# One encoder layer on one core: weight-copy transfers in program order, token quarters of 272, and a last down-product with its depth loop outermost

## The chip, the core and the metric

The kernel runs as one program on one of the cores of a Trainium2 chip. The metric is the device time of one execution in microseconds (us). Before the change it is 1176.99 us, the median of 3 runs (1176.88 to 1177.64). In the tables PE is TensorE, PEld its weight loads, DVE VectorE, ACT ScalarE, POOL GpSimd and SP SyncE, on which most DMAs are issued.

## The reference

One layer over 1024 prompt tokens and 64 tokens of a running stream, 1088 in all, all in float32 (states and small outputs left out):

```
hn = rmsnorm(x, g_pre1); z = hn @ w_in            # 1024 -> gate_a | xa | u | v, 512 each
h  = rg_lru(causal_dwconv(xa, width 4), ...)      # recurrence over tokens, 8 heads
ya = rmsnorm(h * gelu(gate_a), g_out_a)
yb = rmsnorm(spatial_gate(u, layernorm(v), w_s, b_s), g_out_b)
x  = x + rmsnorm(concat(ya, yb) @ w_o, g_post1)   # 1024 -> 1024
up = rmsnorm(x, g_pre2) @ w_up                    # 1024 -> 6144
c  = causal_dwconv(up, width 3)
f  = (gelu(c[..., :3072]) * c[..., 3072:]) @ w_down   # 3072 -> 1024
y  = x + rmsnorm(f, g_post2)
```

## The kernel before

Activations lie transposed: features on the 128 partitions, tokens along the row. Every product is made from three matmuls, since each float32 operand is split into a hi part (a rounded copy, made by ScalarE) and a lo part (the rest, a subtraction on VectorE): hi by hi, hi by lo, lo by hi (`split`, L139 to L144).

The stages on TensorE are, in order: the v product in two passes (tile `vps`, L284 and L290), each over 8 depth blocks k of x; the other three quarters of the input projection (`ps`, L425); the output projection (`ops`, L650) over four token quarters of QW = 274 columns; two pairs of up-projection blocks (`pps`, L775); the other 22 pairs as seven products each (`up`, L906; a product is 24 matmuls, 4 depth blocks by 3 split parts by 2 banks, 3,696 in all), on sums of token quarters; the down projection as seven products of six steps (`dps`, L1067); of those the last product in two column ranges (`lps`, L1067, COLS2). A token row has a gap of 3 columns between the two streams (SG = 1027), for the convolutions. With 4 x 274 = 1096 columns the fourth quarter holds 202 prompt tokens, the gap, 64 sample tokens and 5 columns of nothing: `post1` writes the zeros with GpSimd and cuts its multiplies in two there.

After an up-projection product, ScalarE copies or VectorE adds its two banks into `uraw` (`copy` L920, `add` L925). `gated` makes the convolution and the gate of a pair from it and stores the operand to DRAM (`bd`).

The down projection's weights are w_down blocks and sums of them. Two kinds of sums need w_down[1,0] + w_down[1,1]; that sum is made in DRAM (`sd`) by six copies (L1031, on SP) and six accumulating transfers (L1033, on POOL). They stand in the program text in the loop over the up-projection's pairs, but a scheduler writes each engine's order by when operands are there, and these need nothing: it puts them at the start, on SP between the x loads (`xr`, L323) and the weight loads (`wraw`, L166). A load is followed by a subtraction where the weight is a difference (`wmake`, L1007), then by the split into `whi` and `wlo` (L142). Operands come back from DRAM as `graw` (`bload`) and are split into `gh` and `gl` (`bmake`). The engines' orders are static: each runs its instructions in order.

In the last product each weight tile serves two output blocks. The loop runs over ranges, output blocks m, then the three depth groups kg; weights and operands of a step are made just before (`operand`, L1152). `finish` (L1102) is the work after a column range: a sum of squares over partitions, its inverse root, a broadcast by TensorE, for each of eight blocks a multiply on VectorE (L1112), and a transfer that adds the result onto yT in DRAM (L1113). `finish_last` (L1123) does it for the last range with the gain put in ahead (tile `fg`) and two transfers of four blocks (L1132).

Of the kernel before, what the change touches and what calls it, by code (L numbers as in the profile page):

```python
# [19 lines left out]
QW = 274  # L20
TW = 4 * QW
T = SEQ + DEC
SG = SEQ + GAP
# [20 lines left out]
COLS2 = [(544, 828), (828, 1088)]  # L44
# [23 lines left out]
def layer_kernel(ctx: ExitStack, tc, xT, w_fm, w_v, w_o, w_up, w_down, w_g, w_s, par, bc, yT, small, vn_out):  # L68
# [36 lines left out]
    def qs(q):  # L105
        return slice(q * QW, min(q * QW + QW, T))

    def qw(q):
        return qs(q).stop - q * QW

    def fourth(i, w=QW):
        return slice(i % 4 * QW, i % 4 * QW + w)

    def packed(n, dt, name, w):
        tiles = [big_tile(dt, name=name) for _ in range((n + 3) // 4)]
        return [tiles[i // 4][:, fourth(i, w)] for i in range(n)], tiles

    def v4(t, w=QW):
        return t.rearrange("p (c t) -> p c t", c=4)[:, :, :w]
# [80 lines left out]
    def rstd_tail(head, out):  # L200
# [8 lines left out]
        nc.scalar.activation(out, bp[:, :w], AF.Copy)  # L209
        return bp[:, :w]  # L210
# [349 lines left out]
    def gate_tile_chunks(t):  # L560
        g = big_tile(name="gt")[:, :T]
        h = hst[t]

        def evac(c, ps):
            nc.vector.tensor_tensor(g[:, qs(c)], ps, rbt[:, qs(c)], op=ALU.mult)
            nc.scalar.activation(g[:, qs(c)], g[:, qs(c)], AF.Gelu_apprx_tanh)
            nc.vector.tensor_tensor(h[:, qs(c)], h[:, qs(c)], g[:, qs(c)], op=ALU.mult)
            sat3[c] = acc_tile(qw(c), "sat3")
# [26 lines left out]
    def y_split(c, half):  # L595
        head = rstd_head((sat if half == 0 else sbt)[:, qs(c)], DA, None if half else sat3[c])
        yield
        w = qw(c)
# [3 lines left out]
        for i in range(4):  # L602
            k = half * 4 + i
            y = (hst[i] if half == 0 else s[i])[:, qs(c)]
            nc.vector.scalar_tensor_tensor(y, y, pv("g_out", k), rr, op0=ALU.mult, op1=ALU.mult)
            yh[k, c], yl[k, c] = th[:, fourth(i, w)], tl[:, fourth(i, w)]
            split(yh[k, c], yl[k, c], y)
            if i == 1:
                yield
# [25 lines left out]
    def o_mm(c, gens=()):  # L635
        pss = {}
        w = qw(c)
# [15 lines left out]
        mix, tiles = packed(8, F32, "mix", w)  # L653
# [35 lines left out]
    def load_x(c):  # L689
        xs, tiles = packed(8, F32, "xs", qw(c))  # L690
        for g in range(2):
            nc.sync.dma_start(v4(tiles[g], qw(c)), xT[4 * g:4 * g + 4, :, qs(c)].rearrange("k p t -> p k t"))
        return xs, tiles

    def split_b(name, c, src):
        hi, lo = big_tile(F32R, name="bh"), big_tile(F32R, name="bl")
# [4 lines left out]
    def post1(c, mix, tiles, ssq):  # L701
        w = qw(c)
# [7 lines left out]
        for m in range(KD):  # L710
# [3 lines left out]
            if m % 4 == 3:  # L714
                g = m // 4
                nc.sync.dma_start(yT[:, 4 * g:4 * g + 4, qs(c)], v4(xt[g], w))
            if m == 3:
                yield
        if c == 3:
            n = SEQ - c * QW  # L720
            for t in tiles:
                nc.gpsimd.memset(v4(t)[:, :, n:n + GAP], 0.0)
                nc.gpsimd.memset(v4(t)[:, :, w + GAP:QW], 0.0)
            cuts = ((slice(0, n), slice(0, n)), (slice(n, w), slice(n + GAP, w + GAP)))
        else:
            cuts = ((slice(0, w), slice(0, w)),)
# [7 lines left out]
        for m in range(KD):  # L734
            f = tiles[m // 4][:, fourth(m)]
            for d, g in cuts:
                nc.vector.scalar_tensor_tensor(f[:, g], xs[m][:, d], pv("g_pre2", m), rr2[:, d],
                                               op0=ALU.mult, op1=ALU.mult)
# [26 lines left out]
    def pre_up(n):  # L765
# [4 lines left out]
        def one(i, c):  # L770
# [6 lines left out]
            nc.scalar.activation(raw[i][:, fourth(c)], ps, AF.Copy)  # L777
# [133 lines left out]
    def up_pair(j, hooks=()):  # L911
        xg, xv = big_tile(name="uraw"), big_tile(name="uraw")
        q1, q2, q3, q4 = ([x[:, fourth(2 * c + r)] for c in range(2)]
# [3 lines left out]
        def copy(dst, src):  # L917
            for c in range(2):
                with tc.high_priority(offset=PRI):
                    nc.scalar.activation(dst[c], src[c], AF.Copy)  # L920

        def add(dst, src, p):
            for c in range(2):
                with tc.high_priority(offset=PRI):
                    nc.vector.tensor_tensor(dst[c], src[c], p[c], op=ALU.add)  # L925
# [25 lines left out]
        add(q1, b0, q1)  # L951
# [8 lines left out]
        add(q4, b2, q4)  # L960
# [5 lines left out]
        def last():  # L966
            product(j, 6, b2, False)
            add(q2, b2, q2)
# [17 lines left out]

    def wload(n):
        if n >= NDS:
            return
        p, i = n // 6, n % 6  # L990
# [9 lines left out]
    def wmake(n):  # L1000
        if n >= NDS:
            return
        p, i = n // 6, n % 6
# [17 lines left out]
    for j in range(NPRE, NF):  # L1021
# [39 lines left out]
    def down_mm(dst, cols, n, k, mi, first, last):  # L1061
        hi, lo = wq[n]
        bh, bl = bq[n // 6 * 6 + n % 3 * 2 + k // 2]
# [38 lines left out]
    def finish(cols):  # L1102
# [7 lines left out]
        for m in range(KD):  # L1110
            f = facc[m][:, cols]
            nc.vector.scalar_tensor_tensor(f, f, pv("g_post2", m), rr, op0=ALU.mult, op1=ALU.mult)  # L1112
            nc.gpsimd.dma_start(yT[:, m, cols], f, accum_op=ALU.add)  # L1113
# [3 lines left out]
    fg = {}  # L1117

    def scale_f(m, cols):
        nc.scalar.activation(fg[m // 4][:, m % 4, :], facc[m][:, cols], AF.Copy, scale=pv("g_post2", m))  # L1120

    def finish_last(cols, more):
        w = cols.stop - cols.start  # L1123
        head = rstd_head(ssqt[0][:, cols], D, more)
        scale_f(3, cols)
        rr = tmp_tile(w, name="rrf")
        bp = rstd_tail(head, rr)
        for g, q in ((1, nc.sync), (0, nc.scalar)):
            for m in range(4):
                f = fg[g][:, m, :]  # L1130
                nc.vector.tensor_tensor(f, f, bp, op=ALU.mult)
            nc.gpsimd.dma_start(yT[:, 4 * g:4 * g + 4, cols], fg[g], accum_op=ALU.add)  # L1132

    def down_step(n):
        p, mp, kg = n // 6, n % 6 // 3, n % 3
        for mi in range(2):
# [3 lines left out]
            for k in range(4):  # L1140
                down_mm(dps[m], CC, n, k, mi, kg == 0, kg == 2)
# [9 lines left out]
    last_p = len(DOWN) - 1  # L1151
    def operand(n):  # L1152
        wmake(n + 4)
        bmake(n + 6)
        wload(n + 5)
        bload(n + 7)

    for n in range(6 * last_p):
        if n == 6 * last_p - 6:
# [3 lines left out]
        operand(n)  # L1163
# [3 lines left out]
        if n == 1:  # L1167
            nc.gpsimd.dma_start(small, sm)
    for r, (lo, hi) in enumerate(COLS2):
        cols = slice(lo, hi)  # L1170
        w = hi - lo
        if r == 1:
            for g in range(2):
                fg[g] = big_tile(name="fg")[:, :4 * w].rearrange("p (m t) -> p m t", m=4)
            for m in range(4, KD):
                scale_f(m, cols)
        for m in range(4):
            ps = bank_tile("lps")[:, :w]
            for kg in range(3):
                n = 6 * last_p + m // 2 * 3 + kg  # L1180
                if r == 0 and m % 2 == 0:
                    operand(n)
                for k in range(4):
                    down_mm([ps], [(lo - HT, hi - HT)], n, k, m % 2, kg == 0, kg == 2)
                tick2()
            f = facc_cols(m, lo, hi)
            with tc.high_priority(offset=PRI):
                nc.vector.tensor_tensor(f, ps, f, op=ALU.add)
# [89 lines left out]
```

## Time and profile before

| | us |
|---|---|
| median of 3 runs | 1176.99 |
| the profiled execution | 1176.07 |
| its span, first to last instruction | 1173.9 |
| PE busy (share of the span) | 1132.0 (96%) |
| PEld busy | 1109.0 (94%) |
| DVE busy | 841.0 (72%) |
| ACT busy | 534.2 (46%) |
| POOL busy | 172.0 (15%) |

The trace is of one execution. The shares are means over stages with different limits, so the stages are looked at one by one below. A line of the waits names who was waited for; the chain of waits is followed back from the last instruction; a timeline row may hold several equal instructions (x6), whose time is then from the start of the first to the end of the last.

### The profile page before, as it was taken

The numbers are of one execution on the slowest core, as the hardware profiler recorded it, in microseconds if no ns is written. First come the engines' busy times: TensorE is split into PE (matmuls) and PEld (weight loads), VectorE is DVE, ScalarE is ACT, GpSimd is POOL, SyncE is SP. The second block draws the span as 40 slices with busy tenths as digits, with TensorE's granted clock in tenths as the row PEclk, the third lists the DMA queues.
The fourth block names the chain that finished last, engine by engine and source line by source line (L and its number), as shares of the span: only waits on it lengthen the run. The fifth ranks groups of instructions, "written<-read, shape, count | busy, mean of one in ns | idle before, by whom it ended". The sixth has DMA issues, their size and how long they took to land.

```text
span 1173.9 us, 20616 instructions
## 1 busy us (share of the span) xinstructions
PE 1132.0 (96%) x8420; PEld 1109.0 (94%) x8420; DVE 841.0 (72%) x1363; ACT 534.2 (46%) x876; POOL 172.0 (15%) x291
## 2 busy tenths in 40 slices
PE   6899999999998999999999999999999999999984
PEld 4689999999998999999999999999999999999984
DVE  4568585865678789877877787787789365855753
ACT  4521675645444464444444454454456432523331
POOL 1030001110001113220211111112013000001213
PEclk8999999999999999999999999999999999999987
DMA  9811111140224123221322332232256779555925
GB/s 316 211 54 42 36 37 36 37 129 1 78 96 166 41 79 130 103 103 57 129 99 74 107 114 85 80 130 81 69 207 232 282 256 338 180 213 179 274 31 77
DMA packets 51566, 146.38 MB, mean 125 GB/s; under 512 B 5520, under 2 KB 21392, under 8 KB 51376
## 3 DMA queue, kind: packets, MB, share of 16 engines
q1 hardware_dynamic: 35936, 110.66, 27.3%
q0 software_dynamic: 15312, 34.27, 10.4%
q8 instruction: 66, 1.08, 0.4%
q14 instruction: 28, 0.23, 0.1%
q10 hardware_dynamic: 224, 0.14, 0.0%
HBM read 109.34 MB, written 41.99 MB: 129 GB/s over the span
## 4 chain that ended last, share of the span: by engine, by line
PE 86%; issue 6%; DMA 3%; DVE 2%; POOL 1%; ACT 1%; SPq 0%; POOLq 0%; DVEq 0%; ACTq 0%
PE up L906 40%; PE dps L1067 16%; PE ps L425 12%; PE ops L650 7%; PE pps L775 4%; PE vps L290 2%; DMA xr<-in_xT_dram 1%; DMA wraw<-in_w_v_dram 1%; PE gps L511 1%; PE bp L205 1%; POOL out_dram L1113 1%; PE sp L382 1%; PE st L193 1%; DVE gl L142 1%; ACT whi L140 1%
## 5 line engine op out<-in xcount | busy, mean ns | idle before, releaser
L906 PE MATMUL up<-bh,wop 128*128 128x274 f32 x2464 | 472.3, 290 | 0.0
L906 PEld LDWEIGHTS up<-bh,wop 128*128 128x128 f32 x2464 | 389.1, 189 | 1.7 <-ACT uraw L920 0.9
L906 PE MATMUL up<-bl,wop 128*128 128x274 f32 x1232 | 356.4, 289 | 0.0
L906 PEld LDWEIGHTS up<-bl,wop 128*128 128x128 f32 x1232 | 233.4, 189 | 0.0
L1067 PE MATMUL dps<-gh,whi 128*128 128x272 f32 x576 | 119.7, 289 | 0.7 <-ACT whi L140 0.5
L1067 PE MATMUL dps<-gl,whi 128*128 128x272 f32 x576 | 119.6, 288 | 0.0
L1067 PE MATMUL dps<-gh,wlo 128*128 128x272 f32 x576 | 119.1, 288 | 0.1
L142 DVE TENSOR_TENSOR wlo<-wraw,whi 128x1024 fp32r<-128x1024 f32 x70 | 85.4, 1221 | 35.4 <-ACT whi L140 34.8
L140 ACT ACTIVATE whi<-wraw 128x1024 fp32r<-128x1024 f32 x70 | 73.4, 1055 | 73.8 <-DVE wraw L1007 56.9
L140 ACT ACTIVATE wop<-wsum 128x512 fp32r<-128x512 f32 x88 | 53.0, 626 | 107.7 <-DVE wsum L862 105.3
L920 ACT ACTIVATE uraw<-up 128x274 f32<-128x274 f32 x176 | 65.6, 389 | 64.2 <-PE up L906 63.9
L1067 PEld LDWEIGHTS dps<-gh,whi 128*128 128x128 f32 x576 | 90.3, 188 | 1.1 <-ACT whi L140 0.7
L1067 PEld LDWEIGHTS dps<-gh,wlo 128*128 128x128 f32 x576 | 90.2, 188 | 0.4 <-DVE wlo L142 0.3
L1067 PEld LDWEIGHTS dps<-gl,whi 128*128 128x128 f32 x576 | 90.6, 188 | 0.0
L806 DVE SCALAR_TENSOR_TENSOR yg<-uraw,pt,yg 128x1090 f32<-128x1090 f32 (+1 forms) x48 | 64.8, 1350 | 26.2 <-ACT yg L804 26.2
L925 DVE TENSOR_TENSOR uraw<-up,uraw 128x274 f32<-128x274 f32 x132 | 56.3, 438 | 33.5 <-PE up L906 30.6
L650 PE MATMUL ops<-yh,whi 128*128 128x274 f32 (+1 forms) x256 | 75.3, 294 | 0.0
L650 PE MATMUL ops<-yl,whi 128*128 128x274 f32 (+1 forms) x256 | 73.8, 288 | 0.0
L650 PE MATMUL ops<-yh,wlo 128*128 128x274 f32 (+1 forms) x256 | 73.8, 288 | 0.0
L425 PE MATMUL ps<-xh,whi 128*128 128x364 f32 (+3 forms) x296 | 69.5, 328 | 0.0
L806 DVE SCALAR_TENSOR_TENSOR yv<-uraw,pt,yv 128x1090 f32<-128x1090 f32 (+1 forms) x48 | 64.6, 1346 | 4.8 <-ACT yv L804 4.7
L425 PE MATMUL ps<-xh,wlo 128*128 128x364 f32 (+3 forms) x296 | 67.6, 324 | 0.0
(220 smaller groups left out, 2143.7 us busy)
## 6 DMA issues: line engine op xcount, KB each, us to landing
wraw<-in_w_up_dram SPq DMA_DIRECT2D x48, 512.0 KB, 4.1
graw<-bd SPq DMA_DIRECT2D x42, 544.0 KB, 6.4
wraw<-in_w_down_dram SPq DMA_DIRECT2D x42, 512.0 KB, 5.4
bd<-yg POOLq DMA_DIRECT2D x36, 272.0 KB, 3.4
wraw<-sd SPq DMA_DIRECT2D x18, 512.0 KB, 5.4
bd<-ta POOLq DMA_DIRECT2D x24, 272.0 KB, 3.2
bd<-tb POOLq DMA_DIRECT2D x24, 272.0 KB, 3.0
wraw<-in_w_fm_dram SPq DMA_DIRECT2D x12, 512.0 KB, 3.6
```

The lines of the kernel that those rows point to most:

```text
L140: nc.scalar.activation(hi, src, AF.Copy, scale=1.0 if scale is None else scale)
L142: nc.vector.tensor_tensor(lo, src, hi.bitcast(F32), op=ALU.subtract)
L193: nc.tensor.matmul(st[:sb, b:b + 1], ssq[:, o:o + sb], ones[:, 0:1], start=True, stop=more is None)
L290: nc.tensor.matmul(ps[b][:vrows(b), :], a[:, vcols(b)], wt[:, o:o + 512], start=False, stop=(k == KD - 1 and q == 2))
L425: nc.tensor.matmul(ps[c], wt[:, k * P:(k + 1) * P], at[k][:, cols], start=(k == 0 and q == 0), stop=(k == KD - 1 and q == 2))
L650: nc.tensor.matmul(ps, wt[:, i * 256 + mi * P:i * 256 + (mi + 1) * P], a[k, c], start=(first and i == 0 and j == 0), stop=(last and i == 3 ...
L775: nc.tensor.matmul(ps, wt[:, k * P:(k + 1) * P], a[k, c], start=(k == 0 and j == 0), stop=(k == KD - 1 and j == 2))
L806: nc.vector.scalar_tensor_tensor(y[:, d:TG], x[:, :TG - d], tap(2 - d), y[:, d:TG], op0=ALU.mult, op1=ALU.add)
L906: nc.tensor.matmul(dst[c], wt[:, k * P:(k + 1) * P], at[:, fourth(k)], start=(start and k == 0 and q == 0), stop=(k == 3 and q == 2), skip ...
L920: nc.scalar.activation(dst[c], src[c], AF.Copy)
L925: nc.vector.tensor_tensor(dst[c], src[c], p[c], op=ALU.add)
L1067: nc.tensor.matmul(ps, wt[:, k * 256 + mi * P:k * 256 + (mi + 1) * P], at[:, o + a:o + b], start=(first and k == 0 and q == 0), stop=(last ...
```

## The change

There are five parts.

- QW becomes 1088 / 4 = 272 and the quarters have no gap. The gap is made where `uraw` is written: a new `gapq` gives the fourth quarter as two pieces of 208 and 64 columns, each with its own instruction on ScalarE or VectorE. The zeros and cuts of `post1` go.
- The copies and accumulations into `sd` are kept in program order, so they stay where the text has them.
- COLS2, the ranges of the last product, are 274 and 270 wide instead of 284 and 260.
- In the last product's first range the depth group is the outermost loop, over four banks; the weights come in the order that this needs (`w_index`), and operands a step earlier.
- The ranges of the last product load the earlier yT values (`load_xn`), add on VectorE and store plainly, from SP and ACT queues. The two ranges before (COLS1) still use accumulating transfers. In `finish_last` the gain is applied in place and the broadcast is read from the bank without a copy.

```diff
-QW = 274
+QW = T // 4
-COLS2 = [(544, 828), (828, 1088)]
+COLS2 = [(544, 818), (818, 1088)]
...
+    def gapq(x, q):
+        n = SEQ - q * QW
+        if q < 3:
+            return [(x[:, qs(q)], slice(0, QW))]
+        return [(x[:, q * QW:SEQ], slice(0, n)), (x[:, SG:TG], slice(n, QW))]
...
-            nc.sync.dma_start(sd[0, i], w_down[1, 0, i])
+            tc.keep_in_program_order(nc.sync.dma_start(sd[0, i], w_down[1, 0, i]))
         if 1 <= i < 7:
-            nc.gpsimd.dma_start(sd[0, i - 1], w_down[1, 1, i - 1], accum_op=ALU.add, max_dma_last_dim=1024)
+            tc.keep_in_program_order(nc.gpsimd.dma_start(sd[0, i - 1], w_down[1, 1, i - 1], accum_op=ALU.add,
+                                                         max_dma_last_dim=1024))
...
+    def w_index(n):
+        i = n % 6
+        return i if n < NDS - 6 else i % 2 * 3 + i // 2
...
+    def load_xn(cols):
+        w = cols.stop - cols.start
+        xn = [big_tile(name="xn")[:, :4 * w].rearrange("p (m t) -> p m t", m=4) for _ in range(2)]
+        for g in range(2):
+            nc.sync.dma_start(xn[g], yT[:, 4 * g:4 * g + 4, cols])
+        return xn
...
-        bp = rstd_tail(head, rr)
-        for g, q in ((1, nc.sync), (0, nc.scalar)):
-            for m in range(4):
-                f = fg[g][:, m, :]
-                nc.vector.tensor_tensor(f, f, bp, op=ALU.mult)
-            nc.gpsimd.dma_start(yT[:, 4 * g:4 * g + 4, cols], fg[g], accum_op=ALU.add)
+        bp = rstd_tail(head)
+        for m in (4, 5, 6, 7, 0, 1, 2, 3):
+            f = facc[m][:, cols]
+            x = xn[m // 4][:, m % 4, :]
+            nc.vector.tensor_tensor(f, f, bp, op=ALU.mult)
+            nc.vector.tensor_tensor(x, x, f, op=ALU.add)
+            if m % 2 == 1:
+                (nc.sync if m % 4 == 1 else nc.scalar).dma_start(yT[:, m - 1:m + 1, cols],
+                                                                 xn[m // 4][:, m % 4 - 1:m % 4 + 1, :])
...
+        if r == 0:
+            for kg in range(2):
+                for m in range(4):
+                    mm(m, kg)
+                if kg == 0:
+                    wmake(n0 + 5)
...
+            for kg in range(2 if r == 0 else 0, 3):
+                mm(m, kg)
```

The first place is the queue of SP right behind the load of the parameters (`pt`). Before:

```order
L304 DMA pt<-in_par_dram 128x432
L1031 DMA sd<-in_w_down_dram 16x8192 x2
L323 DMA xr<-in_xT_dram 128x1088
L1031 DMA sd<-in_w_down_dram 16x8192 x2
L323 DMA xr<-in_xT_dram 128x1088
L1031 DMA sd<-in_w_down_dram 16x8192 x2
L166 DMA wraw<-in_w_v_dram 128x1024 x3
```

After:

```order
L308 DMA pt<-in_par_dram 128x432
L327 DMA xr<-in_xT_dram 128x1088 x2
L169 DMA wraw<-in_w_v_dram 128x1024 x3
L169 DMA wraw<-in_w_g_dram 128x1024
L327 DMA xr<-in_xT_dram 128x1088 x2
L169 DMA wraw<-in_w_fm_dram 128x1024
```

The six copies have moved out from between the loads; they stand one by one among the loads of the up-projection's weights, far behind.

The second place is VectorE around the end of the second-to-last product, where the operands of the last one are made. L1007 (after: L1008) subtracts two weight tiles, L142 (L145) makes a lo part of a weight or an operand, L1076 (L1078) adds a bank of the product before, L1112 (L1121) is a multiply of a finish. Before:

```order
L1007 TENSOR_TENSOR wraw<-wraw 128x1024
L142 TENSOR_TENSOR wlo<-wraw,whi 128x1024
L142 TENSOR_TENSOR gl<-graw,gh 128x1088
L1076 TENSOR_TENSOR facc<-dps,facc 128x272 x4
L218 TENSOR_TENSOR ssqt<-ssqt,sq 128x272 x2
L1112 SCALAR_TENSOR_TENSOR facc<-facc,pt,rrf 128x272
L1076 TENSOR_TENSOR facc<-dps,facc 128x272 x3
L1007 TENSOR_TENSOR wraw<-wraw 128x1024
L1076 TENSOR_TENSOR facc<-dps,facc 128x272
L218 TENSOR_TENSOR ssqt<-ssqt,sq 128x272 x2
L1112 SCALAR_TENSOR_TENSOR facc<-facc,pt,rrf 128x272
L142 TENSOR_TENSOR wlo<-wraw,whi 128x1024
```

After:

```order
L1078 TENSOR_TENSOR facc<-dps,facc 128x272 x4
L222 TENSOR_TENSOR ssqt<-ssqt,sq 128x272 x2
L1121 SCALAR_TENSOR_TENSOR facc<-facc,pt,rrf 128x272 x2
L1008 TENSOR_TENSOR wraw<-wraw 128x1024
L1078 TENSOR_TENSOR facc<-dps,facc 128x272 x3
L145 TENSOR_TENSOR wlo<-wraw,whi 128x1024
L1078 TENSOR_TENSOR facc<-dps,facc 128x272
L145 TENSOR_TENSOR gl<-graw,gh 128x1088
L222 TENSOR_TENSOR ssqt<-ssqt,sq 128x272 x2
L1121 SCALAR_TENSOR_TENSOR facc<-facc,pt,rrf 128x272 x6
L1008 TENSOR_TENSOR wraw<-wraw 128x1024
L145 TENSOR_TENSOR wlo<-wraw,whi 128x1024
```

Before, one weight subtraction stood ahead of the product's first four sums and the second among the next four; now the first stands among those later sums, and the second behind the six multiplies.

The third place is the end of VectorE's order, with the last sums of squares (L218, L222), the last bank (L1188), the inverse root (L184) and the finishes. Before:

```order
L218 TENSOR_TENSOR ssqt<-ssqt,sq 128x260
L1188 TENSOR_TENSOR facc<-lps,facc 128x260
L184 TENSOR_SCALAR v<-st 87x3
L1131 TENSOR_TENSOR fg<-fg,bp 128x260 x8
```

After (L1126 and L1144 add onto the loaded yT values, L1143 multiplies by the broadcast):

```order
L1121 SCALAR_TENSOR_TENSOR facc<-facc,pt,rrf 128x274
L1143 TENSOR_TENSOR facc<-facc,bp 128x270
L1126 TENSOR_TENSOR xn<-xn,facc 128x274
L1144 TENSOR_TENSOR xn<-xn,facc 128x270
L1143 TENSOR_TENSOR facc<-facc,bp 128x270 x2
L1144 TENSOR_TENSOR xn<-xn,facc 128x270 x2
```

Behind the inverse root stand now eight multiplies and eight sums in turn, with the rest of the first range's finish between the first of them.

## Rows read from the trace of the kernel before

**Rows 1.** Busy time by stage: stretch, length, busy us (count) per engine, PEclk, DMA, GB/s

```profile
0.00:57.00 57.00, 41.04 (x145) 30.81 (x146) 29.76 (x44) 27.59 (x35) 7.50 (x14) 0.91 0.94 271
...
416.00:888.00 472.00, 472.00 (x3693) 470.29 (x3692) 384.26 (x598) 229.07 (x403) 85.94 (x166) 1.00 0.29 100
...
1108.70:1156.60 47.90, 41.49 (x304) 39.84 (x302) 29.82 (x49) 15.34 (x25) 14.38 (x17) 0.93 0.39 61
1156.60:1173.90 17.30, 2.10 (x19) 1.71 (x17) 3.36 (x10) 1.21 (x3) 3.59 (x4) 0.61 0.61 85
```

**Rows 2.** Waits of PE: waited for, us in total, times, longest

```profile
PE vps L290 <- ACT whi L140: 5.4, 1, 5.4
PE vps L290 <- ACT xh L140: 5.4, 3, 2.3
```

**Rows 3.** Chain of waits, its first transfers: start, us, what

```profile
4.19 6.25 DMA sd<-in_w_down_dram
10.46 13.75 DMA wraw<-in_w_v_dram
26.29 14.49 DMA xr<-in_xT_dram
```

**Rows 4.** Busy time in 2 to 50 us, columns as in Rows 1

```profile
2.00:50.00 48.00, 34.04 (x114) 25.12 (x115) 28.21 (x40) 24.59 (x30) 6.67 (x7) 0.89 1.08 317
```

**Rows 5.** DMA issues of sd: queue, count, KB each, median us to landing

```profile
sd<-in_w_down_dram SPq DMA_DIRECT2D x6, 512.0 KB, 7.9
sd<-in_w_down_dram POOLq DMA_DIRECT2D x6, 512.0 KB, 19.4
```

**Rows 6.** Timeline of PE in the v product: start, us, what

```profile
11.26 0.40 PE L284 MATMUL vps<-w0l,x0h 128*128 128x512 f32 x1
...
52.75 1.56 PE L290 MATMUL vps<-whi,xh 128*128 128x512 f32 x6
...
56.95 0.39 PE L284 MATMUL vps<-w0h,x0h 128*128 128x512 f32 x1
```

**Rows 7.** Timeline of PE in the last input-projection tile, 274 and 266 columns

```profile
237.47 0.29 PE L425 MATMUL ps<-xh,whi 128*128 128x274 f32 x1
...
246.60 0.29 PE L425 MATMUL ps<-xh,whi 128*128 128x266 f32 x1
...
249.44 0.29 PE L425 MATMUL ps<-xh,wlo 128*128 128x266 f32 x1
```

**Rows 8.** Chain of waits, up and down projection

```profile
415.38 472.70 PE up L906 x3696
888.08 108.28 PE dps L1067 x863
```

**Rows 9.** Groups by form, ScalarE's copies: busy, mean ns, idle before

```profile
L920 ACT ACTIVATE uraw<-up 128x274 f32<-128x274 f32 x176 | 65.6, 389 | 64.2 <-PE up L906 63.9
```

**Rows 10.** Timeline of PE, the last product's longest wait

```profile
1120.64 0.84 PE L1067 MATMUL lps<-gh,whi 128*128 128x284 f32 x2 [4.01 <-ACT gh L140]
```

**Rows 11.** Timeline of DVE around the start of the last product

```profile
1105.14 1.48 DVE L1076 TENSOR_TENSOR facc<-dps,facc 128x272 f32<-128x272 f32 x4 [1.15 <-PE dps L1067]
...
1114.80 2.56 DVE L1112 SCALAR_TENSOR_TENSOR facc<-facc,pt,rrf 128x272 f32<-128x272 f32 x6
1117.28 1.22 DVE L1007 TENSOR_TENSOR wraw<-wraw 128x1024 f32<-128x1024 f32 x1
1119.62 1.22 DVE L142 TENSOR_TENSOR wlo<-wraw,whi 128x1024 fp32r<-128x1024 f32 x1 [1.12 <-ACT whi L140]
...
1121.97 1.22 DVE L1007 TENSOR_TENSOR wraw<-wraw 128x1024 f32<-128x1024 f32 x1
```

**Rows 12.** Timeline of DVE, the last finish

```profile
1161.45 2.77 DVE L1131 TENSOR_TENSOR fg<-fg,bp 128x260 f32<-128x260 f32 x8 [2.60 <-ACT rrf L209]
```

**Rows 13.** DMA issues: the last range's stores, and the stores of xs

```profile
out_dram<-fg POOLq DMA_DIRECT2D x2, 520.0 KB, 6.9
out_dram<-xs SPq DMA_DIRECT2D x2, 532.0 KB, 3.0
```

More of the change, by code (lines that the diff above doesn't have):

```diff
@@ L19 @@
 GAP = 3
-QW = 274
-TW = 4 * QW
 T = SEQ + DEC
+QW = T // 4
+TW = 1096
 SG = SEQ + GAP
@@ L105, in qs, with fourth, packed, v4 @@
     def qs(q):
[L106 to L119, printed above, removed]
+        return slice(q * QW, q * QW + QW)
+    def fourth(i):
+        return slice(i % 4 * QW, i % 4 * QW + QW)
+    def packed(n, name):
+        tiles = [big_tile(name=name)[:, :T] for _ in range((n + 3) // 4)]
+        return [tiles[i // 4][:, fourth(i)] for i in range(n)], tiles
+    def v4(t):
+        return t.rearrange("p (c t) -> p c t", c=4)
+    def gapq(x, q):
[3 more added lines that the diff above has]
+        return [(x[:, q * QW:SEQ], slice(0, n)), (x[:, SG:TG], slice(n, QW))]
     gp = const.tile([P, 8], F32, name="gp")
@@ L208, in rstd_tail @@
                 tc.keep_in_program_order(mm)
-        nc.scalar.activation(out, bp[:, :w], AF.Copy)
+        if out is not None:
+            nc.scalar.activation(out, bp[:, :w], AF.Copy)
         return bp[:, :w]
@@ L776, in one @@
                                      start=(k == 0 and j == 0), stop=(k == KD - 1 and j == 2))
-            nc.scalar.activation(raw[i][:, fourth(c)], ps, AF.Copy)
+            for dst, cut in gapq(raw[i], c):
+                nc.scalar.activation(dst, ps[:, cut], AF.Copy)
         for i0 in range(0, n, 2):
@@ L912, in up_pair @@
         xg, xv = big_tile(name="uraw"), big_tile(name="uraw")
-        q1, q2, q3, q4 = ([x[:, fourth(2 * c + r)] for c in range(2)]
+        q1, q2, q3, q4 = ([gapq(x, 2 * c + r) for c in range(2)]
                           for x, r in ((xg, 0), (xg, 1), (xv, 0), (xv, 1)))
@@ L1150, in layer_kernel @@
     dps = {}
[L1151 to L1159, printed above, removed]
+    n0 = NDS - 6
+    for n in range(n0):
+        if n == n0 - 6:
             for c in COLS1:
@@ L1162, in layer_kernel @@
         down_step(n)
-        operand(n)
+        wmake(n + 4)
+        if n < n0 - 6:
+            bmake(n + 6)
+            bload(n + 7)
+        elif n == n0 - 6:
+            bload(n0 + 1)
+            bmake(n0)
+            bload(n0 + 2)
+            bmake(n0 + 1)
+        elif n < n0 - 1:
+            bload(n + 8)
+            bmake(n + 7)
+        wload(n + 5)
         if n == 0:
@@ L1177, in layer_kernel @@
         for m in range(4):
[L1178 to L1185, printed above, removed]
+            for kg in range(2 if r == 0 else 0, 3):
+                mm(m, kg)
             f = facc_cols(m, lo, hi)
             with tc.high_priority(offset=PRI):
-                nc.vector.tensor_tensor(f, ps, f, op=ALU.add)
+                nc.vector.tensor_tensor(f, pss[m], f, op=ALU.add)
                 if r == 1 and m == 3:
@@ L1196, in layer_kernel @@
         if r == 0:
-            gens2.append(finish(cols))
+            gens2.append(finish(cols, xn))
     while gens2:
         tick2()
-    finish_last(cols, more)
+    finish_last(cols, xn, more)
 def _lay(inp, np):
```

93 lines of the change are left out of this document (48 added, 45 removed).

## The prediction

> **What bounds the kernel now.** I read the busy time by stage first [rows 1]. TensorE is busy for 472.0 of 472.0 us in the up-projection (416 to 888 us), so there a change counts only through the matmuls' own pace. Idle time stands in three places: in the first 57 us TensorE works 41.0 us (and at 0.91 of its clock), in the last product (1108.7 to 1156.6) 41.5 of 47.9 us, and after the last matmul 17.3 us pass. The waits say what for: in the start TensorE waits for ScalarE's hi halves of weights and of x, 5.4 us once and 5.4 us in three pieces [rows 2]. The chain of waits leads on from there: ScalarE waited for transfers, and the chain's first transfer is a copy into sd of 6.25 us, followed by a w_v load of 13.75 us and an xr load of 14.49 us [rows 3]. So the start is bound by the DMA, and the six weight copies and their six accumulations, which nothing needs before the down projection, stand in it.
>
> **The copies out of the start.** In 2 to 50 us the DMA was busy throughout (share 1.08) and moved 317 GB/s, 15.2 MB; the twelve sd transfers are 12 x 512 KB = 6.3 MB of that [rows 4, 5]. In the new SP order the first xr and w_v loads stand directly behind pt. The loads left, 15.2 - 6.3 = 8.9 MB, take 8.9 / 0.317 = 28 us, so the last xr lands near 30 us; at the 271 GB/s of the first 57 us [rows 1] it would be 33 us, near 35. TensorE's side: k = 0 ends at 11.5; seven more k of 18 matmuls follow. Six matmuls in a row take 1.56 us, the last with its 0.39 us of pipeline, so (1.56 - 0.39) / 5 = 0.233 us each, 126 x 0.233 = 29.4 us, and the pass ends at 40.9 instead of 56.95 [rows 6]: 16 us less. The last k starts at 36.7 there; its x needs to land 2.6 us earlier (a hi and a lo split of 1.2 and 1.35 us), at 34. By the first rate it does, by the second it is a microsecond late. I take 15 us, with ends 11 (loads at 230 GB/s) and 16. TensorE's order is the same in both programs up to the output projection, and no wait is seen behind 57 us that an earlier start would uncover, so I keep all of it. The copies reappear one per pair in the up-projection, where the DMA share is 0.29 [rows 1]: hidden, and if that cover failed, one price stands among the rivals.
>
> **Quarters of 272.** 3,696 matmuls of the up-projection and 384 of the pairs before it have 274 columns and get 272; in the gate tile and the output projection three quarters shrink by 2 and the fourth grows by 6, so their sum stays. Bounds for the 4,080: from 274 to 266 columns the pace goes from (246.60 - 237.47) / 72 = 126.8 ns to (249.44 - 246.60) / 23 = 123.5 ns [rows 7], 0.41 ns a column, so 0.83 ns x 4,080 = 3.4 us. The other end is the row of equal width: 274 wide in the up-projection 472.70 / 3696 = 127.9 ns, 272 wide in the down projection 108.28 / 863 = 125.5 ns [rows 8], 2.4 ns x 4,080 = 9.9 us. The 272 row is the nearer one in shape and length, though it uses each weight for two chunks; I take 1.7 ns, 7 us. The Trainium skill (TensorE: Matmul & The Clock Gate, Back-to-back issue gap) has the gap at full clock as columns / 2.4 plus 2.5 ns, which would make 272 columns 115.8 ns and the gain 0.83 ns x 4,080 = 3.4 us. By that rule the level is 10 ns too low for either row here, so the rows decide.
>
> The fourth quarter's evacuation now comes in two pieces (208 and 64 columns): per pair two more ScalarE and two more VectorE instructions. A whole one is 0.389 us and was waited for by nobody: ScalarE sat 64.2 us idle ahead of them, for TensorE [rows 9]. I cost them at nothing; exposed, each pair would pay up to four such, 1.6 us (the rival below). The masked GpSimd memsets and eight of the split multiplies go; nobody on the path waited for them: nothing.
>
> **The last product.** The old order waited 4.01 us for gh and ran at half clock (1.2 GHz) after it [rows 10], of 6.4 us idle in that stretch. Depth outermost spreads the need: weight tile w needs to be there every 3 us (24 matmuls of 0.1255). But VectorE's order decides when the tiles are there. For each of the six it first subtracts (L1007), then ScalarE makes hi, then VectorE lo and one gl: from one subtraction to the next 1121.97 - 1117.28 = 4.69 us, hi ready 2.3 us and lo ready 3.5 us after the subtraction's start [rows 11]. In the new order the first of these subtractions stands behind the sums of the product before, where the old order had it ahead of them, and the second behind six multiplies of the finish. From the product's start (0): the four sums begin at -3.6 (1105.14), 1.4 us to the next; two ssqt sums 0.7, two multiplies 0.8; subtraction 1 at -0.6, hi at 1.7, then three sums of the last step, lo at 2.9, a sum, a gl, two ssqt sums and the six multiplies (2.5, L1112 in [rows 11]) to 7.6; subtraction 2 at 7.6, hi 9.9, lo 11.1; tile 3 lo at 15.8, tile 4 at 20.5, tile 5 (no gl between) at 24.0. TensorE: waits 1.7 + 0.7 for tile 1, is through with it at 5.4, waits 4.5 + 0.7 for tile 2, and from 11.1 on has 260 of 288 matmuls left, less the four done: 5.5 us on tile 2 and tile 1's second range reach 16.6, past tile 3; every later tile is in time. 216 matmuls more x 0.1255 = 27.1: 43.7, with 1.05 for the small matmuls of the finishes (an estimate for the 304 - 288 of [rows 1]) 44.7, and 2.5 for the half clock behind a wait as long as the old one: 47.2 against 47.9. I take -0.6, with +2 and -3 (no half clock) as ends. So the waits come back in another place.
>
> **The tail.** Two accumulating stores leave, the second once the eight multiplies end at 1164.2, and take 6.9 us to land [rows 12, 13]; 4.3 us from the last matmul to the broadcast stay. New: no copy of the broadcast (0.5 us), then 8 multiplies and 8 sums and one sum left of the other range, 17 x 0.34 (2.77 / 8) = 5.8 us from 1161.0 to 1166.8, and the last plain store, 270 KB, by the nearest row (532 KB, 3.0 us) down at 1169.8, plus the 2 us that passed at the end of the old run: 1171.8 against 1173.9, -2.1. Ends: -3.2 (the store lands in 2), -0.8 (4.3 us). The first range's plain stores lie ahead of that, beside matmuls. The Trainium skill (DMA: Bandwidth & Descriptors, Anatomy of one DMA) has 2.0 us plus bytes / 436 GB/s for a transfer queued by GpSimd: 3.2 us for 520 KB. By that the old stores would be down at 1167.5 and the new sums would make the tail about 2 us longer; the rows have 6.9, so I don't follow it.
>
> **Sum.** -15.0 - 7.0 - 0.6 - 2.1 = -24.7 us. The profiled execution took 1176.07 us (span 1173.9), 0.9 below the median of 1176.99: 1151.4 for such a one, 1152.3 for a median.
>
> **Rivals.** (a) The last product runs without waits, because the static order costs less than I read: 288 x 0.1255 + 1.05 = 37.2 us, -10.7 instead of -0.6: 1142. For it: all loads of the six tiles are issued before 1109. Against: the order itself; chance 0.12. (b) Transfers still bind the start: loads move slower than copies do, below 190 GB/s alone, the last x lands near 47 / 1.15 = 41 us and half of the 15 goes: 1160. For it: the 317 GB/s are counted with copies in them. Chance 0.13. (c) Slower: the fourth quarter's two-piece evacuation holds TensorE. Place: each of 22 pairs, where the bank's next product waits for the second piece. Price: up to 1.6 us a pair, 35 us; from 1.1 us a pair (24.7 / 22) it decides, at the full price 1187. For it: VectorE and ScalarE are strictly in order with 1.3 us instructions between. Against: a whole product, 24 matmuls or 3 us, lies between an evacuation and the bank's next use, and TensorE had no gap in 472 us. Chance 0.04. (d) The copies, now in SP's queue ahead of w_up loads, hold these six times by some 4 us each, and all is given back: 1176; chance 0.03, since w_up loads are issued a whole pair ahead.
>
> **How the numbers follow.** My forecast has 0.68. Its own range is 1146 to 1159: start 11 to 16, width 3.4 to 9.9, last product +2 to -3, tail -0.8 to -3.2, not all at one end. The range 1144 to 1161 takes in (b). About 0.2% is what the timing can tell from no change. Faster by more: 0.68 + 0.12 + 0.13 = 0.93; within: 0.03, (d); slower: 0.04, (c).
>
> **What would show it.** Right: no sd transfer before the up-projection, the first matmul of the second pass near 41 us, the up-projection's 3,696 matmuls in 464 to 469 us without gaps, two waits of 2 to 5 us in the last product on the weight halves, and last stores landing in about 3 us. Wrong: an xr wait left after 30 us, waits on uraw in the up-projection, or a last product under 42 us.

## The result, and the profile after

The changed kernel takes 1158.84 us (median of 4 runs, 1158.54 to 1160.74) against 1177.32 us of the kernel before on the same chip: ratio 0.9846, 95% interval 0.9829 to 0.9864. Against the 1176.99 us that the forecast started from it is 18.1 us less. The profiled execution took 1158.54 us, with a span of 1156.8 us.

Busy time by stage of the changed kernel, columns as in [rows 1]; the cuts are the start of the up-projection (400.26) and of the down projection (866.87), the end of the latter, and the last product's end:

```profile
0.00:45.00 45.00, 38.89 (x156) 30.47 (x157) 31.63 (x50) 29.53 (x39) 1.14 (x8) 1.00 0.58 204
45.00:400.26 355.26, 352.27 (x2502) 344.52 (x2501) 253.39 (x482) 170.29 (x298) 38.82 (x62) 1.00 0.20 65
400.26:866.87 466.61, 466.61 (x3699) 464.50 (x3698) 384.93 (x641) 232.20 (x449) 91.16 (x172) 1.00 0.36 115
866.87:1094.50 227.63, 222.99 (x1753) 221.58 (x1751) 134.94 (x170) 87.39 (x115) 23.61 (x26) 0.99 0.72 244
1094.50:1142.40 47.90, 42.17 (x303) 41.01 (x302) 30.77 (x50) 14.96 (x23) 7.55 (x9) 0.93 0.39 102
1142.40:1156.80 14.40, 2.65 (x19) 2.25 (x17) 9.46 (x27) 0.95 (x2) 1.04 (x1) 0.62 0.44 155
```

The start has the DMA at 0.58 and 204 GB/s in 45 us, where [rows 1, 4] had it full. The up-projection still has no idle time and is 6.1 us shorter [rows 8]. What was not forecast stands in the fourth line: the down projection, of which the kernel before has this row:

```profile
888.08:1108.74 220.66, 219.90 (x1753) 219.15 (x1752) 136.78 (x170) 87.40 (x113) 21.07 (x26) 1.00 0.72 254
```

The busy time rose by 3.1 us (matmuls at half clock behind a wait, so the granted clock is 0.99) and the idle time from 0.8 to 4.6 us. Up to the last product's first matmul, at 1096.54, another 2.0 us pass; they are the first of the two waits that the forecast had in the last product, and are counted there. So the balance, stage by stage:

| | before | after | difference | forecast |
|---|---|---|---|---|
| up to the up-projection | 415.4 | 400.3 | -15.1 | -15 (and -0.7 of pace) |
| up-projection | 472.7 | 466.6 | -6.1 | -6.3 |
| down projection without the last product | 220.7 | 227.6 | +7.0 | 0 |
| last product | 47.9 | 47.9 | 0.0 | -0.6 |
| from there to the end | 17.3 | 14.4 | -2.9 | -2.1 |
| span | 1173.9 | 1156.8 | -17.1 | -24.7 |

TensorE's waits in the changed kernel (who was waited for: us, times, longest) answer to [rows 2]: the start's waits for whi and xh are gone, and the down projection has new ones.

```profile
PE lps L1069 <- ACT whi L143: 4.6, 2, 2.6
...
PE dps L1069 <- ACT whi L143: 3.0, 1, 3.0
PE vps L294 <- DVE xl L147: 1.5, 1, 1.5
PE dps L1069 <- DVE gl L145: 1.5, 2, 1.0
```

VectorE ahead of the longest new one, in the changed kernel:

```profile
968.23 1.28 DVE L145 TENSOR_TENSOR gl<-graw,gh 128x1088 fp32r<-128x1088 f32 x1
974.02 0.79 DVE L1078 TENSOR_TENSOR facc<-dps,facc 128x272 f32<-128x272 f32 x2 [4.51 <-PE dps L1069]
976.52 0.79 DVE L1078 TENSOR_TENSOR facc<-dps,facc 128x272 f32<-128x272 f32 x2 [1.71 <-PE dps L1069]
977.23 1.22 DVE L1008 TENSOR_TENSOR wraw<-wraw 128x1024 f32<-128x1024 f32 x1
979.62 1.23 DVE L145 TENSOR_TENSOR wlo<-wraw,whi 128x1024 fp32r<-128x1024 f32 x1 [1.18 <-ACT whi L143]
```

The weight that the next product begins with is subtracted at 977.23, behind four sums of which the last two could not start before TensorE had ended the product at 976.5; TensorE then waits until its hi part is there, 979.6. In the last product the same engine reads, as forecast from [rows 11]:

```profile
1094.19 1.22 DVE L1008 TENSOR_TENSOR wraw<-wraw 128x1024 f32<-128x1024 f32 x1
...
1099.93 2.56 DVE L1121 SCALAR_TENSOR_TENSOR facc<-facc,pt,rrf 128x272 f32<-128x272 f32 x6
1102.41 1.22 DVE L1008 TENSOR_TENSOR wraw<-wraw 128x1024 f32<-128x1024 f32 x1
```

### The profile page after: what moved, and what is told of

Its sections match the earlier page's. It is cut to its first block, busy times and chain, and to the rows that moved or that the text cites. A ratio compares the mean times of both kernels' runs of the same rounds, so it can differ in the third digit from the quotient of the medians.

```text
span 1156.8 us, 20691 instructions
## 1 busy us (share of the span) xinstructions
PE 1125.6 (97%) x8420; PEld 1104.3 (95%) x8420; DVE 845.1 (73%) x1415; ACT 535.3 (46%) x923; POOL 163.3 (14%) x277
## 4 chain that ended last, share of the span: by engine, by line
PE 91%; DVE 5%; issue 2%; ACT 1%; DMA 0%; POOL 0%; SPq 0%; POOLq 0%; DVEq 0%; ACTq 0%
PE up L901 40%; PE dps L1069 17%; PE ps L429 12%; PE ops L654 7%; PE pps L769 4%; PE vps L294 3%; PE lps L1069 3%; PE gps L515 1%; PE bp L208 1%; PE sp L386 1%; ACT whi L143 1%; PE st L196 1%; DVE wraw L1008 1%; DVE gl L145 1%; DVE bl L145 0%
## 5 line engine op out<-in xcount | busy, mean ns | idle before, releaser
L901 PE MATMUL up<-bh,wop 128*128 128x272 f32 x2464 | 466.0, 289 | 0.0
L901 PE MATMUL up<-bl,wop 128*128 128x272 f32 x1232 | 354.8, 288 | 0.0
L145 DVE TENSOR_TENSOR wlo<-wraw,whi 128x1024 fp32r<-128x1024 f32 x70 | 85.1, 1220 | 27.5 <-ACT whi L143 27.2
L143 ACT ACTIVATE whi<-wraw 128x1024 fp32r<-128x1024 f32 x70 | 73.2, 1055 | 67.7 <-DVE wraw L1008 56.4
L916 ACT ACTIVATE uraw<-up 128x272 f32<-128x272 f32 (+2 forms) x220 | 67.9, 344 | 53.8 <-PE up L901 53.5
L922 DVE TENSOR_TENSOR uraw<-up,uraw 128x272 f32<-128x272 f32 (+2 forms) x176 | 58.8, 364 | 32.2 <-PE up L901 29.9
L654 PE MATMUL ops<-yh,whi 128*128 128x272 f32 x256 | 75.1, 293 | 0.0
L654 PE MATMUL ops<-yh,wlo 128*128 128x272 f32 x256 | 73.7, 288 | 0.0
L654 PE MATMUL ops<-yl,whi 128*128 128x272 f32 x256 | 73.6, 288 | 0.0
L429 PE MATMUL ps<-xh,whi 128*128 128x364 f32 (+2 forms) x296 | 69.4, 328 | 0.0
L188 POOL TENSOR_TENSOR rs<-v,mhalf 91x3 f32<-91x3 f32 (+2 forms) x20 | 24.6, 1229 | 308.2 <-DVE v L187 308.2
L429 PE MATMUL ps<-xh,wlo 128*128 128x364 f32 (+2 forms) x296 | 67.7, 324 | 0.0
```

Source lines behind the costliest of these rows:

```text
L143: nc.scalar.activation(hi, src, AF.Copy, scale=1.0 if scale is None else scale)
L145: nc.vector.tensor_tensor(lo, src, hi.bitcast(F32), op=ALU.subtract)
L188: nc.gpsimd.tensor_tensor(out, v[:n[0], :n[1]], mhalf[:n[0], :n[1]], op=ALU.pow)
L429: nc.tensor.matmul(ps[c], wt[:, k * P:(k + 1) * P], at[k][:, cols], start=(k == 0 and q == 0), stop=(k == KD - 1 and q == 2))
L654: nc.tensor.matmul(ps, wt[:, i * 256 + mi * P:i * 256 + (mi + 1) * P], a[k, c], start=(first and i == 0 and j == 0), stop=(last and i == 3 ...
L901: nc.tensor.matmul(dst[c], wt[:, k * P:(k + 1) * P], at[:, fourth(k)], start=(start and k == 0 and q == 0), stop=(k == 3 and q == 2), skip ...
```

## The experiments

After the result, the theory for the missing 7 us was a line of the diff that the prediction passed over; it belongs to none of the change's five parts. In the down projection's loop the kernel before calls `wload(n + 5)` and then `bload(n + 7)`; the changed one calls `bload` first, in every step. Each weight load then stands behind an operand load in SP's queue. Expectations below that speak of 9 us count the last product's first wait of 2.0 us with the down projection. The rivals: the copies cost time again later; the quarters or the plain stores do it by buffers or DMA traffic.

**e1_copies.** The kernel before with one part of the change.

```diff
-            nc.sync.dma_start(sd[0, i], w_down[1, 0, i])
+            tc.keep_in_program_order(nc.sync.dma_start(sd[0, i], w_down[1, 0, i]))
...
-            nc.gpsimd.dma_start(sd[0, i - 1], w_down[1, 1, i - 1], accum_op=ALU.add, max_dma_last_dim=1024)
+            tc.keep_in_program_order(nc.gpsimd.dma_start(sd[0, i - 1], w_down[1, 1, i - 1], accum_op=ALU.add,
+                                                         max_dma_last_dim=1024))
```

> The kernel before, with only the six copies and six accumulations into sd kept in program order. Theory (the start was bound by the DMA, and the copies cost it about 15 us): 1177.3 - 15.3 = 1162.0 (the trace of the changed kernel has the up-projection's pairs begin 15.3 us earlier), with the up and down projections as long as before (472.7 and 220.8 us). Rival 1 (the copies cost time again where they now stand, among the up-projection's weight loads, or the down projection pays for them): start 15 us shorter, but the down projection some 9 us longer, 1171. Rival 2 (something else in the change shortened the start): 1177.

Measured: 1162.57 us against 1176.56, ratio 0.9874 (0.9845 to 0.9904), -14.0. The up-projection (472.6 us) and the down projection are as before, in the windows of this run:

```profile
402.06:874.70 472.64, 472.61 (x3699) 470.71 (x3698) 385.16 (x599) 229.93 (x404) 90.80 (x172) 1.00 0.36 114
874.70:1095.30 220.60, 219.82 (x1753) 219.01 (x1752) 136.73 (x171) 87.34 (x113) 21.18 (x26) 1.00 0.73 254
```

The copies are hidden where they stand now; both rivals fall.

**e2_width.** The kernel before with the quarters of 272.

```diff
-QW = 274
+QW = T // 4
...
-            nc.scalar.activation(raw[i][:, fourth(c)], ps, AF.Copy)
+            for dst, cut in gapq(raw[i], c):
+                nc.scalar.activation(dst, ps[:, cut], AF.Copy)
```

> The kernel before, with only the quarters of 272, the two-piece evacuation and what goes with it. Theory (TensorE paces the up-projection and the two-piece evacuation is free): up-projection 466.6 us instead of 472.7, the pair stage and the output projection within 1 us, down projection as before; 1177.3 - 6.5 = 1170.8, without a gap of TensorE in the up-projection. Rival (the down projection's 9 us come from this part, through the buffers and the gate work that the smaller quarters move): up-projection 466.6 but down projection about 229, 1180.

Measured: 1168.35 against 1176.56, ratio 0.9928 (0.9904 to 0.9952), -8.2; up-projection 466.5 us without idle time, down projection 220.8. The two-piece evacuation holds nobody, and the down projection's loss is not from here.

**e3_wload_first and e4_bload_first.** The order of the two loads, undone in the changed kernel (e3) and done in the kernel before (e4).

```diff
         if n < n0 - 6:
             bmake(n + 6)
+            wload(n + 5)
             bload(n + 7)
...
-        wload(n + 5)
+        if n >= n0 - 6:
+            wload(n + 5)
```

> The changed kernel, with the weight loads ahead of the operand load again in the down projection's steps up to the second-to-last product (program text only, 29 steps). Theory (the changed order of these two loads makes each weight land later, so that the static order puts the weight subtractions behind the sums that wait for TensorE; in the third and fourth product this costs 4.0 and 1.7 us): those two products take 36.8 and 37.1 us as before instead of 40.8 and 38.8, the last two stay; 1158.8 - 5.7 = 1153.1. Rival (the loss comes from the buffers, the plain stores' loads or DMA contention): products 3 and 4 stay near 40.8 and 38.8, 1158.8.

> The kernel before, with only the operand load put ahead of the weight loads in the down projection's steps up to the second-to-last product. Theory (load order): the third and fourth product take 40.8 and 38.8 us as in the changed kernel instead of 36.8 and 37.1, 1177.3 + 5.7 = 1183.0. Rival (not the load order): 1177.3, products as before.

Measured: e3 1146.62 against 1176.56, ratio 0.9737 (0.9704 to 0.9770), 12.2 less than the changed kernel. e4 1188.1, ratio 1.0089 (1.0057 to 1.0120), 11.5 more than the kernel before. Products 3 and 4 of the down projection take 36.8 and 37.1 us in e3, and 40.8 and 38.4 in e4, which has the 3.0 us wait of the changed kernel at the same place. So the load order is the cause, in both kernels. It cost twice what I expected, since I had read it in products 3 and 4 alone: e3's down projection is 7.0 us shorter, 1.4 of it in the sixth product, and its last product takes 44.3 us instead of 47.9, without the first of the two waits. (The pair stage of e3 was 1.2 us shorter by its clock; the last section tells of it.)

VectorE in e3, at the place shown above for the changed kernel:

```profile
971.01 0.79 DVE L1078 TENSOR_TENSOR facc<-dps,facc 128x272 f32<-128x272 f32 x2 [3.84 <-PE dps L1069]
971.72 1.22 DVE L1008 TENSOR_TENSOR wraw<-wraw 128x1024 f32<-128x1024 f32 x1
973.51 0.79 DVE L1078 TENSOR_TENSOR facc<-dps,facc 128x272 f32<-128x272 f32 x2 [0.58 <-PE dps L1069]
```

The subtraction stands between the two pairs of sums, ahead of the pair that waits for TensorE's last matmuls; in the changed kernel, and in e4, it stands behind both pairs. So the order of the loads changed VectorE's static order. How the scheduler comes from the one to the other is not shown.

SP's own waits, in the changed kernel between 866 and 1096 us (operand loads L977, weight loads L998), then in e3 between 865 and 1086 us:

```profile
SPq L977 <- PE dps L1069: 85.2, 18, 9.6
SPq L998 <- PE dps L1069: 53.0, 15, 11.1
```

```profile
SPq L998 <- PE dps L1069: 101.1, 26, 14.6
SPq L977 <- PE dps L1069: 22.2, 8, 5.8
```

The queue waits for buffers that TensorE still reads. In the changed kernel mostly the operand load waits at the head of the queue, with the weights behind it; in e3 mostly the weight load does.

**e10_pin.** Is it that the weights land late, or that the static order has their subtraction behind the sums? The loads keep the changed kernel's order, and at six places the subtraction is held ahead of the sums.

```diff
...
-        down_step(n)
-        wmake(n + 4)
+        first = n % 3 == 2 and DOWN[(n + 4) // 6][1] in ("S2", "S3", "S4")
+        if first:
+            wmake(n + 4)
+            with tc.issue_after(subs[n + 4]):
+                down_step(n)
+        else:
+            down_step(n)
+            wmake(n + 4)
```

> The changed kernel with its loads in their own order (operand ahead of weights), but with VectorE's subtraction of the next weight pair held ahead of the sums at the end of each half product (six places). Theory (the weights lie in place long before; what costs the time is the subtraction's place behind sums that wait for TensorE): the third and fourth product fall from 40.8 and 38.8 us to about 37, the down projection from 229.8 to 222 or less, the whole from 1158.8 to 1151. Rival (the weights land late, because they are loaded behind the operand): the held sums now wait for the subtraction and nothing is won, 1159 or more.

Measured: 1141.87 against 1176.96, ratio 0.9702 (0.9681 to 0.9723), 17 less than the changed kernel. VectorE, from the subtraction for the fourth product's first step on, and behind the cut that for its fourth step:

```profile
956.40 1.22 DVE L1009 TENSOR_TENSOR wraw<-wraw 128x1024 f32<-128x1024 f32 x1
957.53 0.78 DVE L1079 TENSOR_TENSOR facc<-dps,facc 128x272 f32<-128x272 f32 x2
...
974.40 1.23 DVE L1009 TENSOR_TENSOR wraw<-wraw 128x1024 f32<-128x1024 f32 x1 [3.25 <-DMA wraw<-in_w_down_dram]
975.54 0.78 DVE L1079 TENSOR_TENSOR facc<-dps,facc 128x272 f32<-128x272 f32 x2
976.68 0.79 DVE L1079 TENSOR_TENSOR facc<-dps,facc 128x272 f32<-128x272 f32 x2 [0.36 <-PE dps L1070]
```

and its down projection:

```profile
868.40:1087.40 219.00, 219.00 (x1754) 219.00 (x1753) 138.94 (x168) 89.64 (x115) 30.27 (x25) 1.00 0.70 248
```

Not one idle microsecond, with the loads in the changed kernel's order. The place behind the sums is what turns the order of the loads into a wait. The changed kernel's own trace speaks against the rival too. The weight that its fourth product begins with is the first one behind the six of the third product, whose differences POOL stores into DRAM, the last at 966.20 us; its two loads (SP's queue, and their issue to landing) are these:

```profile
945.50 2.74 SPq L998 DMA_DIRECT2D wraw<-in_w_down_dram  x2
wraw<-in_w_down_dram SPq DMA_DIRECT2D x2, 512.0 KB, 6.1
```

They had landed at 953.4 us, 24 us before the subtraction at 977.23 that TensorE waited for. In e10 VectorE does wait for a transfer, at 974.40, but for a weight that TensorE reaches only at 994.6, and TensorE waits for nothing.

**e6_both.** e1 and e2 together, nothing of the last product.

> The kernel before, with the copies in program order and the quarters of 272, and with none of the rest (last product, its stores and the down projection's loop as before). Theory (the parts add up): -14.5 from the copies and -8 from the quarters as they measured alone, 1176.6 - 22 = 1154 (forecast by the prediction's terms: 1155). Rival (the parts share one cover, say the weight loads of the up-projection): 1160 or more. Against the kernel that loads weights first (1146.6) it also tells what the rest of the change is worth: 7 to 8 us.

Measured: 1154.32 against 1177.86, ratio 0.9798 (0.9770 to 0.9827), -23.5: the two parts add up (14.0 + 8.2 = 22.2). Against e3 the last product, its stores and the tail are worth 7 to 8 us, once the loads are in their old order.

**e7_ahead.** e3 with weights loaded ahead also in the last six steps before the last product, and in the last five of them a step earlier.

```diff
+        if n <= n0 - 5:
+            wload(n + 5)
+        if n >= n0 - 5:
+            wload(n + 6)
...
-        wload(n + 5)
...
-    wload(n0 + 5)
```

> The changed kernel with the weight loads first in all of the down projection, and in the last product each weight pair loaded one step earlier. Theory (the last product's wait of 3.3 us and the half clock behind it come from the weight subtraction's place, which follows the load): the subtractions stand ahead of the sums and the finish's multiplies, the wait goes, the last product takes 38 to 40 us instead of 44.3, and the whole 1146.6 - 5 = 1141.5. Rival (VectorE's total work there sets it, 24 us of splits in 27 us): another wait of about 3 us appears for a lo part, 1146.

Measured: 1141.14 against 1177.86, ratio 0.9693 (0.9667 to 0.9719), 5.5 less than e3. The last product of e3 and of e7, windows:

```profile
1085.80:1130.10 44.30, 40.37 (x303) 39.22 (x302) 29.00 (x52) 13.04 (x21) 7.96 (x9) 0.96 0.40 100
```

```profile
1086.60:1125.60 39.00, 38.34 (x303) 37.78 (x301) 31.97 (x60) 12.60 (x21) 7.89 (x9) 1.00 0.51 117
```

The wait and the lower clock are gone. VectorE has more to do in less time, and it is enough; the rival falls.

**e8_tail.** e3 with accumulating transfers at the very end.

```diff
-            nc.vector.tensor_tensor(f, f, bp, op=ALU.mult)
-            nc.vector.tensor_tensor(x, x, f, op=ALU.add)
+            nc.vector.tensor_tensor(x, f, bp, op=ALU.mult)
...
+                nc.gpsimd.dma_start(yT[:, m - 3:m + 1, cols], xn[m // 4], accum_op=ALU.add)
```

> The changed kernel with the weight loads first (1146.6), and the last range's plain stores replaced by two accumulating transfers of four blocks each, without loading yT and without the eight sums. Theory (an accumulating transfer takes 6.9 us where a plain store takes about 3, and the eight sums cost 2.8): the time from the last bank's sum to the end grows from 14.3 to 17 us, 1149. Rival (the sums cost what the stores save): 1146.6, within 0.5.

Measured: 1150.68 against 1177.86, ratio 0.9773 (0.9749 to 0.9797), 4.1 more than e3; from the last product's end to the end of the span 17.7 us instead of 14.6, so 3.1 of it here and the rest in earlier stages. The last stores (queue, count, KB each, median us to landing), in e8 and in the changed kernel:

```profile
out_dram<-xn POOLq DMA_DIRECT2D x2, 540.0 KB, 7.0
```

```profile
out_dram<-xn SPq DMA_DIRECT2D x2, 270.0 KB, 2.4
out_dram<-xn ACTq DMA_DIRECT2D x2, 270.0 KB, 2.2
```

The two accumulating transfers of 540 KB, issued 1.5 us apart, take 6.1 and 8.0 us, much as the two of 520 KB of [rows 13]. By the Trainium skill (DMA: Bandwidth & Descriptors, Anatomy of one DMA), 2.0 us plus bytes / 436 GB/s, an estimate for one is 3.3 us; what was measured disagrees with that.

**e9_shift.** Why 272 columns are faster than 274 (e5, the same with last ranges of 276 and 268 columns, gave no result): e3 with the operands of the up-projection 8 bytes further in their rows, and both last ranges 272 wide.

```diff
-COLS2 = [(544, 818), (818, 1088)]
+COLS2 = [(544, 816), (816, 1088)]
...
-        hi, lo = big_tile(F32R, name="bh")[:, :T], big_tile(F32R, name="bl")[:, :T]
+        hi, lo = big_tile(F32R, name="bh")[:, 2:T + 2], big_tile(F32R, name="bl")[:, 2:T + 2]
```

> Two changes read in two stages of one run, on the changed kernel with the weight loads first. (1) The operands of the up-projection lie 8 bytes further in their rows, still 272 columns each. Theory A (the 274-column rows lost time because three of four slices did not start on a 64-byte boundary): the pace rises from 125.5 ns to 126.4 or more, the up-projection from 466.7 to 470. Theory B (the number of columns alone sets it): 125.5 ns, 466.7. (2) The last product's ranges are both 272 wide instead of 274 and 270 (127.7 and 125.3 ns). Theory B1 (time goes by columns evenly): 126.5 ns for both. Theory B2 (there is a step behind 272): as 270, 125.3 ns for both, so that a 274-wide matmul costs 2.4 ns more for two columns.

Measured: one run, 1152.65 us. The up-projection of e3 and of e9, windows:

```profile
398.80:865.35 466.55, 466.55 (x3699) 464.42 (x3698) 384.87 (x641) 231.99 (x449) 90.96 (x172) 1.00 0.36 115
```

```profile
400.05:871.72 471.67, 471.67 (x3698) 471.58 (x3698) 385.06 (x641) 231.96 (x449) 90.93 (x172) 1.00 0.35 114
```

Full clock in both, no idle time, the same instructions: 5.1 us for 8 bytes of offset, over all 3,696 matmuls 127.6 ns each instead of 126.2, where 274 columns had 127.9. So 5.1 of the 6.1 us that the narrower quarters save depend on where the rows lie, as theory A has it; its 64 bytes are not shown (the last section has another size). In the last product, from one start to the next at full clock, the two ranges of 272 run at 125.4 and 125.1 ns, where e3's 274 and 270 had 127.3 and 125.3: B2.

**e11_best.** e7, e10's hold and 272-wide last ranges in one kernel.

> What won, together: the changed kernel with weights loaded first in the down projection and a step earlier in the last product, the subtractions held ahead of the sums at six places, and both last ranges 272 wide. Theory (the places left are independent): the down projection 219.2 us instead of 220.7, the last product 38.6 instead of 39.0, 1141.1 - 1.9 = 1139.2. Rival (the subtraction that is held ahead waits where loads now come first): 1141 or more.

Measured: 1139.05 against 1176.11, ratio 0.9687 (0.9670 to 0.9704), 19.8 us less than the changed kernel. Down projection, last product and tail, windows:

```profile
866.80:1085.60 218.80, 218.80 (x1754) 218.80 (x1753) 137.67 (x167) 90.53 (x115) 21.50 (x25) 1.00 0.70 250
1085.60:1124.30 38.70, 37.98 (x303) 37.48 (x302) 30.57 (x62) 12.50 (x23) 7.90 (x9) 1.00 0.69 177
1124.30:1137.20 12.90, 1.87 (x16) 1.63 (x16) 6.23 (x18) 0.95 (x2) 0.85 (x1) 0.69 0.24 86
```

Of the 2 us over e7 the down projection gives 1.7; the difference of the medians is too small against their intervals to call more than likely.

## Why the prediction was right, and where not

The direction was right and the time lies in the range; 18.1 of the forecast 24.7 us came. That it lies in the range, near its slow end, is in part luck: that end was drawn for smaller gains of the terms and for rival (b), slow loads at the start, and the loss came from a stage that neither had.

**The copies** (-15): right in size and reason. The v product ends 14.6 us earlier (65.4 instead of 80.0), in e1 too, and e1 as a whole is 14.0 faster. Its first pass ends at 42.5 instead of the forecast 40.9, with one wait of 1.5 us left and none after it. Rivals (b) and (d) fall with it: from 9 to 21 us the loads moved 402 GB/s, more than the 317 that the forecast took.

**The quarters** (-7): right in size. 1.7 ns a matmul was the value taken, 1.65 was measured in the up-projection (472.70 / 3,696 to 466.61 / 3,696), 6.1 us. The pair stage has 55.3 us (e3) instead of 56.4 at the same granted clock of 1.00; the changed kernel's own trace, at 0.97, has 56.6. The output projection, whose sum was to stay, went from 108.5 to 107.9. The value was picked between bounds of 0.83 and 2.4, and the reason behind the lower one, columns counted evenly, is wrong by e9: the rows it came from differ in their starts in the buffer too. So the size was in part luck. Rival (c) fell: no gap in 466.6 us.

**The last product** (-0.6): the mechanism was read rightly from VectorE's order. Two waits were forecast, 2.4 and 5.2 us; the trace has 2.0 + 0.5 and 2.6. The second tile's hi part was there 10.2 us after the start (1104.77; forecast 9.9), but TensorE, at half clock behind the first wait, came to it 2.2 us later than forecast. The stage took as long as before (47.9 us), which is within the term's bounds. In e3, with the loads in the old order, the first wait is gone, and in e7, with earlier loads, both are: what rival (a) supposed needed another order of the loads.

**The tail** (-2.1): -2.9; e8 gives 3.1 for the plain stores alone. The 6.9 us that the forecast took for the last old store is the median of two, 6.0 and 7.9 us, and the second is the one that ends last; the new last store took 2.2 us where 3.0 was taken.

**The step that failed** is the sum itself: the down projection stood in no term, so it was priced at nothing. It gave back 7.0 us there, and by e3 and e4 the two calls that changed places cost 11.5 to 12.2 us in all. The 4.69 us "from one subtraction to the next" had VectorE's chain rightly as what limits the weights; it was used for the last product alone, while the third and fourth product subtract their weights in the same way, and there the order of the loads decides where the subtraction stands. Without that line (e3) the kernel gains 29.9 us, more than was forecast.

## What to carry to other kernels

The order of two load calls in a loop can change the static order of an engine that runs neither of them. Compare each engine's order before and after in every stage whose loop was touched, and look for an instruction that now stands behind one that waits (a subtraction behind a sum that waits for TensorE is late by that wait, though its operands landed long before). Read a diff for lines that only change places, and price every stage whose loop they stand in. Choose a tile width by where the slices start as well as by how long they are.

## What the runs showed of the hardware

From one start to the next, pauses over 140 ns and stretches at half clock left out, a 272-column float32 matmul of the up-projection took 125.5 ns where its moving rows began at multiples of 1088 bytes (e3) and 127.5 ns with 8 bytes added to each start (e9), at the same granted clock of 1.00. (The pauses, 29 with 2.8 us in e3 and 7 with 0.3 us in e9, are why the stage as a whole lost only 5.1 us.) The other widths fit a charge for each block of 16 bytes (4 columns) that a row touches, counted from the start of the buffer (or of its second half, at byte 2176, a multiple of 16). This is an estimate from the traces, and no run was made to test it:

| columns | first byte | blocks of 16 bytes | ns, trace |
|---|---|---|---|
| 260 | 1136 | 65 | 119.9, last product before |
| 266 | 3288 | 67 | 123.2, input projection before |
| 270 | 1096 | 68 | 125.3, last product of e3 |
| 272 | multiples of 1088 | 68 | 125.5, up-projection of e3 |
| 272 | the same + 8 | 69 | 127.5, up-projection of e9 |
| 274 | multiples of 1096 | 69 | 127.3, up-projection before |
| 284 | 0 | 71 | 131.0, last product before |

That is 1.84 to 1.85 ns a block in each row. With blocks of 8 bytes e9's offset would have changed nothing, and with 32 or 64 bytes the 266 columns would touch as many as the 272 of e3.

The pair stage (384 matmuls, the same code in e3 and e6; in the kernel before with 274 columns) took 55.3 us at a granted clock of 1.00 in e3 and 58.0 at 0.94 in e6, in windows over it, first the kernel before, then e6, then e3:

```profile
359.03:415.38 56.35, 53.34 (x424) 52.68 (x423) 45.48 (x84) 25.94 (x49) 8.33 (x12) 1.00 0.29 101
```

```profile
344.10:402.10 58.00, 55.56 (x424) 54.74 (x423) 45.04 (x77) 26.22 (x53) 7.68 (x9) 0.94 0.27 95
```

```profile
343.50:398.80 55.30, 52.83 (x424) 51.98 (x423) 44.81 (x77) 26.18 (x53) 7.69 (x9) 1.00 0.28 100
```

e6 and e3 have the same waits there, 0.7, 0.7 and, 17 us into the stage, 1.1 us. Behind these e6 passes matmuls at 1.2 GHz and e3 does not, which by itself makes 2.7 us, more than some of the terms above.
